# A fixed order for three engines in the interleaved part of the MLPs, and seven products instead of eight for 7 of 8 K-pairs

## The chip, the cores and the metric

The kernel runs on one core of a Trainium2 chip. The metric is the device time of one execution in microseconds (us); lower is better. The engines are TensorE (PE, with PEld for its weight loads), VectorE (DVE), ScalarE (ACT), GpSimd (POOL) and SyncE (SP, which here only issues DMAs).

## What is computed

A decoder trunk of two layers over 256 tokens with 2048 features, in float32. Each layer is a mixer (the first one latent attention beside an mLSTM, the second one dilated attention) followed by a squared-ReLU MLP; a final norm ends it. The change touches the MLPs only:

```python
D_MODEL, SEQ, D_FF = 2048, 256, 8192

def squared_relu_mlp(h, w1, w2):
    return jnp.square(jax.nn.relu(h @ w1)) @ w2

for layer in range(2):
    x = x + mix(rms_norm(x, norm_mix[layer]))
    x = x + squared_relu_mlp(rms_norm(x, norm_mlp[layer]), mlp_w1[layer], mlp_w2[layer])
```

## The kernel before

**Split numbers.** Every float32 operand is split into a high and a low half (`halves`): ScalarE copies it into the type that TensorE multiplies (`wh`, line 135), VectorE subtracts that copy from the original (`wl`, line 136). A product is then three matmuls (`mm_three`: high by high, high by low, low by high). Weights arrive as 512 KB pieces (`wr`, line 127) through a ring of four buffers; `wh` and `wl` have rings of four too.

**The MLP.** D_FF is cut into four quarters (q). A quarter's hidden features are made in 16 blocks of 128 (`h`). A block is two halves, each with one weight piece, eight matmuls of 512 columns (line 164) and eight of 256 (line 168), all into PSUM bank 3. A block's result is copied out by ScalarE (`bt_h`), added up by VectorE (`hu`), put through ReLU and square by ScalarE, and stored for the second product: two blocks make a K-pair.

**The second product.** It runs over the 8 K-pairs of a quarter for one half of the 2048 output columns at a time; I call the work of one quarter and one column half a stretch. A K-pair can be multiplied with eight products (24 matmuls of 512 columns; `eight`, called twice a pair with 12 each) or, by Strassen's scheme in Winograd's form, with seven (21 matmuls; `seven`). For seven, VectorE first makes sums of weight pieces (`ta`, `tb`) and of activations (`hp`, then split into `pt`). A seven is two steps: the first (nine matmuls) goes into the PSUM tiles m1, m5, m7 (`ym`), the second (twelve) into m6 and three accumulators (`yc`, the output blocks 10, 01 and 00). The fourth accumulator, block 11, is only used by `eight`, and shares bank 3 with the `h` blocks. The four `ym` tiles come from a pool of four buffers. `SEVEN = 6` pairs go by seven, two by eight.

**The order before.** `woven` writes out one and a half seven-steps, then an `h` block, and so on: the twelve seven-steps of a stretch among eight `h` blocks that belong to the next stretch or to the next half of the quarter. Behind the last block come the four `eight` steps. Behind the last seven-step, `early_y` reads the four `ym` tiles (`yp`, `yq` are scratch) and adds to the residual `x`; behind the last eight, `late_y` adds the four accumulators to `x`. That is the order of writing; the framework's scheduler then orders each engine's queue by itself.

There are seven stretches in each layer (the eighth, at the end of each MLP, is written in another way). Layer 0's begin near 402 us, layer 1's near 1469 us.

Of the kernel before, what the change touches and what calls it, by code (L numbers as in the profile page):

```python
# [21 lines left out]
SEVEN = 6  # L22
# [47 lines left out]
def trunk(ctx: ExitStack, tc: tile.TileContext, plan, a, c_first, c_even, c_odd, out):  # L70
# [122 lines left out]
    def steps_seven(pool, H, pairs, w, c, early, late, name="y", hold=()):  # L193
# [12 lines left out]
        def seven(k):  # L206
# [8 lines left out]
            def go_a():  # L215
# [6 lines left out]
                ta = pool.tile([P, 2, 512], F32, name=f"ta{n_w[0]}", tag="ta", bufs=2)  # L222
# [40 lines left out]
        return [seven(k) for k in pairs], [[eight(k, j) for j in range(2)] for k in rest]  # L263

# [759 lines left out]
    def mlp(layer, norm, nxt):  # L1024
# [6 lines left out]
        def evac_h(H):  # L1031
            def make(c):
                box = {}

                def go(f, ac):
                    t = sm.tile([P, 512], F32, name="bt_h", tag="bt", bufs=2)
                    nc.scalar.activation(t, ac, AF.Copy)
                    u = sm.tile([P, S], F32, name="hu", tag="hu", bufs=2)
                    nc.vector.tensor_add(u, t[:, :S], t[:, S:])  # L1039
                    nc.scalar.activation(u, u, AF.Relu)  # L1040
                    if c >= SEVEN:
                        nc.scalar.activation(u, u, AF.Square)
                        H[2 * c + f] = sm.tile([P, 2, S], FR, name="ht", tag="ht", bufs=2 * (NF // 2 - SEVEN))
                        split_to(H[2 * c + f], u)
# [5 lines left out]
                    v = u.rearrange("p (b t) -> p b t", b=NB)  # L1050
                    nc.scalar.activation(dst, v, AF.Square)
                    if f == 1:
                        nc.vector.tensor_tensor(r[:, 4:6, :], r[:, 1:3, :], r[:, 2:4, :], OP.subtract)
                        nc.vector.tensor_tensor(r[:, 6, :], r[:, 5, :], r[:, 1, :], OP.subtract)
                        nc.vector.tensor_tensor(r[:, 7, :], r[:, 0, :], r[:, 6, :], OP.add)
                        pt = sm.tile([P, 2, 8, P], FR, name="pt", tag="pt", bufs=SEVEN)
                        nc.scalar.activation(pt[:, 0], r, AF.Copy)
                        nc.vector.tensor_tensor(pt[:, 1], r, pt[:, 0].bitcast(F32), OP.subtract)
                        H[2 * c], H[2 * c + 1] = (pt, 0), (pt, 1)
                return go  # L1060
            return make

        def early_y(c):
            def go(m1, m5, m6, m7):
                def add(b, j, src):
                    v = x[b][c + j]
                    nc.vector.scalar_tensor_tensor(v, src, scale["s"][:, b:b + 1], v, OP.mult, OP.add)

                p = sm.tile([P, 512], F32, name="yp", tag="yp", bufs=1)
                q = sm.tile([P, 512], F32, name="yq", tag="yq", bufs=1)  # L1070
                nc.scalar.activation(p, m1, AF.Copy)
                add(0, 0, m1)
                nc.vector.tensor_add(p, m6, p)
                nc.vector.tensor_add(q, m7, p)
                nc.vector.tensor_sub(p, m5, p)
                add(1, 0, q)
                nc.vector.tensor_sub(q, m5, q)
                add(0, 1, p)
                add(1, 1, q)
            return go  # L1080

        def late_y(c):
            def go(cc):
                for b, j in ((1, 1), (1, 0), (0, 1), (0, 0)):
                    v = x[b][c + j]
                    nc.vector.scalar_tensor_tensor(v, cc[b, j], scale["s"][:, b:b + 1], v, OP.mult, OP.add)
            return go

        def blocks(q, H):
# [3 lines left out]
            def block(i):  # L1093
                def go():
                    run(steps_feats(X, ("mlp_w1", layer, 0), q * (FF // NQ) + i * P,
                                    lambda f, ac: ev[i // 2](i % 2, ac), n=P, name="h", kt=8, bank=3))
                return go

            ev = [ev(c) for c in range(NF // 2)]
            return [block(i) for i in range(NF)], ev  # L1100

        H = [None] * NF
        hs, ev = blocks(0, H)
        steps = steps_feats(X, ("mlp_w1", layer, 0), 0, ev[0], name="h")
# [5 lines left out]
        for c in range(1, NF // 4):  # L1110
            run(steps_feats(X, ("mlp_w1", layer, 0), c * 256, ev[c], name="h"))
        for q in range(NQ):
            last = q == NQ - 1
            wq = ("mlp_w2", layer, q * (FF // NQ))
            seven, eight = steps_seven(sm, H, list(range(SEVEN)), wq, 0, early_y(0), late_y(0))
            woven(hs[NF // 2:], sum(seven, []))
            run(*eight)
            if last and nxt is None:
                finish(H, wq, early_y(2), scale, sm)
                break  # L1120
            pairs = list(range(3 if last else SEVEN))
            seven, eight = steps_seven(sm, H, pairs, wq, 1024, early_y(2), late_y(2))
            if last:
                nxt.stats(0)
                nxt.stats(1)
                steps = sum([a + b for a, b in zip(seven, eight)] + eight[len(seven):], [])
# [74 lines left out]
```

## Time and profile before

| | |
|---|---|
| time, three runs | 2115.13, 2117.52, 2119.45 us (median 2117.52) |
| profiled execution | 2115.02 us, span of the trace 2113.2 us |
| TensorE busy | 2093.8 us, 99% of the span |
| VectorE busy | 1742.3 us, 82% (90% or more in most slices of the MLPs) |
| ScalarE busy | 1303.7 us, 62% |
| granted TensorE clock | 0.999 of full |
| DMA | 404.5 MB, mean 191 GB/s |

A matmul's bar in the trace holds its way through the array, so the bars of matmuls that follow each other overlap. How long a run of matmuls takes is read from the starts, not from the bars; the same holds, with less overlap, for VectorE.

### The profile page before, as it was taken

The page shows a single profiled execution, that of the slowest core. Times are in us where ns is not written, and L with a number is a line of the kernel's source. Part 1 is how long each engine was busy: PE and PEld are TensorE (multiplying, and loading weights), DVE is VectorE, ACT ScalarE, POOL GpSimd, SP SyncE. Part 2 cuts the span into 40 slices and gives each one's busy share as a digit, 9 for nine tenths or more (in the row PEclk, how much of TensorE's full clock was granted, in tenths as well). Part 3 has the DMA queues.
Part 4 walks back from the last instruction along what each step waited for, and adds up shares of the span by engine and source line. Part 5 has one row for each costly group of instructions (what it writes and reads, how often), then busy time and mean ns, then how long its engine had stood idle before and what let it go on. Part 6 is the DMA issues. An engine that isn't in the chain of part 4 may idle for free.

```text
span 2113.2 us, 29343 instructions
## 1 busy us (share of the span) xinstructions
PE 2093.8 (99%) x10860; PEld 1797.8 (85%) x10860; DVE 1742.3 (82%) x2455; ACT 1303.7 (62%) x1876; POOL 6.1 (0%) x13
## 2 busy tenths in 40 slices
PE   9999999999999999999999999999999999999998
PEld 8998888888888888888888888888888888888886
DVE  5678555889999999999877667568899998999998
ACT  6575445766676666667544444457666666667665
POOL 0000000000000000000000000000000000000000
PEclk9999999999999999999999999999999999999999
DMA  8554455556565566566665555455565665656664
GB/s 295 165 174 158 160 176 187 178 191 216 183 211 197 190 202 204 192 205 195 197 194 174 170 179 170 163 186 178 193 205 194 206 201 188 204 194 200 203 213 162
DMA packets 115296, 404.51 MB, mean 191 GB/s; under 512 B 12944, under 2 KB 13584, under 8 KB 115152
## 3 DMA queue, kind: packets, MB, share of 16 engines
q1 hardware_dynamic: 114048, 400.02, 57.9%
q8 instruction: 85, 1.39, 0.3%
q0 software_dynamic: 384, 1.51, 0.2%
q10 hardware_dynamic: 720, 1.11, 0.1%
q14 instruction: 59, 0.48, 0.1%
HBM read 400.49 MB, written 2.10 MB: 191 GB/s over the span
## 4 chain that ended last, share of the span: by engine, by line
PE 88%; DVE 7%; DMA 2%; issue 1%; ACT 1%; SPq 0%; POOLq 0%; POOL 0%; DVEq 0%; ACTq 0%
PE h L164 21%; PE h L168 11%; PE yc L155 4%; PE yc L156 4%; PE yc L154 4%; PE ym L155 4%; PE ym L156 3%; PE ym L154 3%; DVE wl L136 3%; PE k L164 3%; PE o L154 3%; PE o L156 3%; PE o L155 3%; PE q L164 3%; PE v L154 2%; PE v L156 2%
## 5 line engine op out<-in xcount | busy, mean ns | idle before, releaser
L136 DVE TENSOR_TENSOR wl<-wr,wh 128x1024 fp32r<-128x1024 f32 (+4 forms) x769 | 865.6, 1134 | 259.8 <-ACT wh L135 254.5
L135 ACT ACTIVATE wh<-wr 128x1024 fp32r<-128x1024 f32 (+4 forms) x769 | 753.8, 986 | 515.6 <-PE h L164 136.6
L164 PE MATMUL h<-T,wh 128*128 128x512 f32 x2048 | 511.4, 392 | 1.1 <-ACT wh L135 0.9
L164 PEld LDWEIGHTS h<-T,wh 128*128 128x128 f32 x2048 | 374.5, 188 | 76.0 <-ACT wh L135 2.6
L168 PEld LDWEIGHTS h<-T,wl 128*128 128x128 f32 x2048 | 279.3, 190 | 20.1
L168 PE MATMUL h<-T,wl 128*128 128x256 f32 x2048 | 285.5, 282 | 0.0
L155 PE MATMUL ym<-wl,pt 128*128 128x512 f32 x360 | 142.2, 395 | 1.8 <-DVE wl L136 1.8
L154 PE MATMUL ym<-wh,pt 128*128 128x512 f32 x360 | 140.1, 394 | 0.2 <-ACT wh L135 0.2
L156 PE MATMUL ym<-wh,pt 128*128 128x512 f32 x360 | 140.2, 389 | 0.0
L224 DVE TENSOR_TENSOR ta<-wr,wr 128x1024 f32<-128x1024 f32 x90 | 110.1, 1223 | 33.1 <-DMA wr<-in_mlp_w 32.4
L135 ACT ACTIVATE wh<-ta 128x1024 fp32r<-128x1024 f32 x90 | 95.2, 1058 | 61.0 <-DVE ta L224 60.9
L155 PE MATMUL yc<-wl,pt 128*128 128x512 f32 x318 | 124.0, 390 | 0.0
L154 PE MATMUL yc<-wh,pt 128*128 128x512 f32 x318 | 123.2, 390 | 0.0
L156 PE MATMUL yc<-wh,pt 128*128 128x512 f32 x318 | 122.8, 389 | 0.0
L1040 ACT ACTIVATE hu<-hu 128x256 f32<-128x256 f32 x128 | 52.6, 415 | 99.5 <-DVE hu L1039 99.3
L135 ACT ACTIVATE wh<-tb 128x1024 fp32r<-128x1024 f32 x90 | 94.7, 1052 | 28.5 <-DVE tb L226 28.3
L136 DVE TENSOR_TENSOR wl<-tb,wh 128x1024 fp32r<-128x1024 f32 x90 | 109.7, 1219 | 1.9 <-ACT wh L135 1.7
L136 DVE TENSOR_TENSOR wl<-ta,wh 128x1024 fp32r<-128x1024 f32 x90 | 109.7, 1219 | 0.0
L154 PE MATMUL o<-wh,M 128*128 128x512 f32 x256 | 102.3, 399 | 0.0
L156 PE MATMUL o<-wh,M 128*128 128x512 f32 x256 | 99.8, 390 | 0.0
L155 PE MATMUL o<-wl,M 128*128 128x512 f32 x256 | 99.7, 389 | 0.0
L154 PE MATMUL yc<-wh,ht 128*128 128x512 f32 (+1 forms) x256 | 99.4, 388 | 0.0
(297 smaller groups left out, 3320.9 us busy)
## 6 DMA issues: line engine op xcount, KB each, us to landing
wr<-in_mlp_w SPq DMA_DIRECT2D x512, 512.0 KB, 4.1
wr<-in_od_w_qkv SPq DMA_DIRECT2D x96, 512.0 KB, 4.1
wr<-in_ev_w_in SPq DMA_DIRECT2D x32, 512.0 KB, 3.5
wr<-in_ev_w_out SPq DMA_DIRECT2D x32, 512.0 KB, 3.4
wr<-in_od_w_out SPq DMA_DIRECT2D x32, 512.0 KB, 3.5
wr<-in_ev_w_in SPq DMA_DIRECT2D x24, 344.0 KB, 3.1
wr<-in_ev_w_in SPq DMA_DIRECT2D x15, 364.0 KB, 5.8
wr<-in_mla_w_ukv SPq DMA_DIRECT2D x8, 512.0 KB, 3.7
```

The costliest lines, as they stand in the source:

```text
L135: nc.scalar.activation(hi, raw, AF.Copy)
L136: nc.vector.tensor_tensor(lo, raw, hi.bitcast(F32), OP.subtract)
L154: nc.tensor.matmul(ac, xh, hi, start=first, stop=False)
L155: nc.tensor.matmul(ac, xh, lo, start=False, stop=False)
L156: nc.tensor.matmul(ac, xl, hi, start=False, stop=last)
L164: nc.tensor.matmul(acs[f], hi[:, j, f * P:(f + 1) * P], Ts[j].rearrange("p a t -> p (a t)"), start=first and j == 0, stop=False)
L168: nc.tensor.matmul(acs[f][:, :S], lo[:, j, f * P:(f + 1) * P], Ts[j][:, 0, :], start=False, stop=last and j == n - 1)
L224: nc.vector.tensor_tensor(ta, r0, r1[:, 0:1, :].to_broadcast([P, 2, 512]), OP.add)
L1040: nc.scalar.activation(u, u, AF.Relu)
```

## The change

`SEVEN` is 7, `ta` has one buffer instead of two (in the old form of the second product as well), and the seven stretches of a layer are written as a list of units whose order is fixed for ScalarE, VectorE and TensorE: the scheduler no longer moves their instructions. The lines that carry it:

```diff
-SEVEN = 6
+SEVEN = 7
...
+    def drive(units, left):
+        ahead = [(n, kind, f) for n, u in enumerate(units) for kind, f in u.prep]
+        due = {}
+        for n, u in enumerate(units):
+            first, rest = due.pop(n, ([], []))
+            splits = []
+            while ahead and left.get(ahead[0][1], 1) > 0:
+                _, kind, f = ahead.pop(0)
+                if kind:
+                    left[kind] -= 1
+                splits.append(f)
+            run(first, [f for pair in zip(splits, rest) for f in pair], splits[len(rest):], rest[len(splits):])
+            for d, now, f in u.go() or ():
+                due.setdefault(n + d, ([], []))[not now].append(f)
+            for kind in u.free:
+                left[kind] += 1
...
+            return [Unit([(None, sums), ("w", split(0, lambda: t["r0"])), ("t", split(1, lambda: t["ta"], pool, "t", 3))],
+                         go_a, ["t"]),
+                    Unit([("w", split(3, lambda: t["r1"][:, 1:2, :])),
+                          ("t", split(2, lambda: t["tb"], pool, "t", 3))], go_b, ["w", "w", "t"])]
...
+                due = [(1, True, copy), (1, False, add), (2, False, square)]
+                if c >= SEVEN:
+                    return due + [(3, False, plain)]
+                return due + ([(3, False, sums), (4, False, pair)] if f == 1 else [])
...
+                return [(1, True, both(nc.scalar.activation, p, m1, AF.Copy)),
+                        (1, True, add(0, 0, m1)),
+                        (1, False, both(nc.vector.tensor_add, p, m6, p)),
+                        (1, False, both(nc.vector.tensor_add, q, m7, p)),
+                        (2, False, both(nc.vector.tensor_sub, p, m5, p)),
+                        (2, False, add(1, 0, q)),
+                        (3, False, both(nc.vector.tensor_sub, q, m5, q)),
+                        (3, False, add(0, 1, p)),
+                        (4, False, add(1, 1, q))]
...
-                for b, j in ((1, 1), (1, 0), (0, 1), (0, 0)):
+                return [(1, True, add(b, j)) for b, j in ((1, 0), (0, 1), (0, 0), (1, 1))]
...
-            woven(hs[NF // 2:], sum(seven, []))
-            run(*eight)
+        pattern = "shshshhshshhshs"
+                for what in pattern:
+                    units += (seven if what == "s" else hs).pop(0)
+                units += eight
+        with tc.manual_schedule(engines={mybir.EngineType.PE, mybir.EngineType.Activation, mybir.EngineType.DVE}):
+            drive(units, {"w": 4, "t": 3})
```

`drive` goes through the units. Ahead of each it writes out what came due (`first`, then the others in turn with the splits for coming units), as many splits as there are free buffers of either kind, then the unit's matmuls. A unit returns what follows from it, with the number of units after which it is due. A stretch is now: seven, block, seven, block, seven, two blocks, seven, block, seven, two blocks, seven, block, seven, two eights. I name its units s0a, s0b (the two steps of the first seven), h0a, h0b (the halves of the block behind it), and so on to s6a, s6b, e0, e1, and then s0a of the next stretch.

**VectorE between two stretches, before.** This is the end of layer 0's fourth stretch (a second column half), from the first early addition on: the splits for the two halves of the `h` block that stands behind the last seven (`wl_7104`, `wl_7126`), the other early additions (lines 1067 to 1077; `ym_6428` is m5), and the first of the splits for the four `eight` steps (`wl_7160`).

```order
L1067 SCALAR_TENSOR_TENSOR x_75<-ym_6427,iv_mlp_3681,x_75 128x512
L136 TENSOR_TENSOR wl_7104<-wr_7101,wh_7103 128x1024
L136 TENSOR_TENSOR wl_7126<-wr_7123,wh_7125 128x1024
L1039 TENSOR_TENSOR hu<-bt_h 128x256
L1073 TENSOR_TENSOR yp<-ym_6430,yp 128x512
L1074 TENSOR_TENSOR yq<-ym_6429,yp 128x512
L1075 TENSOR_TENSOR yp<-ym_6428,yp 128x512
L1067 SCALAR_TENSOR_TENSOR x_79<-yq,iv_mlp_3681,x_79 128x512
L1067 SCALAR_TENSOR_TENSOR x_76<-yp,iv_mlp_3681,x_76 128x512
L1077 TENSOR_TENSOR yq<-ym_6428,yq 128x512
L136 TENSOR_TENSOR wl_7160<-wr_7157,wh_7159 128x1024
L1067 SCALAR_TENSOR_TENSOR x_80<-yq,iv_mlp_3681,x_80 128x512
```

The early additions stand close together, with m5's last reading (the second `yq`) among them. Three more eights' splits and the next stretch's first sums and split follow, and only then the late additions.

**VectorE between two stretches, now.** This is the same place, from the first early addition (due after `s6b`) on; the splits of e0 and e1, one `hu` and s0's sums (`ta`, twice `tb`) stand ahead of it. `wl_7246`, `wl_7253`, `wl_7258` and `wl_7263` are the splits of s0's four pieces (`wr_7209`, `ta`, `wr_7211`, `tb`) in the next stretch, `wl_7281` is that of h0a. The bracket names the engines whose semaphores a row waits for.

```order
L1195 SCALAR_TENSOR_TENSOR x_75<-ym_6506,iv_mlp_3681,x_75 128x512 [waits Activation_49]
L136 TENSOR_TENSOR wl_7246<-wr_7209,wh_7245 128x1024 [waits Activation_49]
L1171 TENSOR_TENSOR hp<-hp 128x256
L1172 TENSOR_TENSOR hp<-hp 128x128 [waits DVE_49]
L1173 TENSOR_TENSOR hp<-hp 128x128 [waits DVE_49]
L136 TENSOR_TENSOR wl_7253<-ta_7213,wh_7252 128x1024 [waits Activation_49]
L1198 TENSOR_TENSOR yp<-ym_6509,yp 128x512
L136 TENSOR_TENSOR wl_7258<-wr_7211,wh_7257 128x512 [waits Activation_49]
L1198 TENSOR_TENSOR yq<-ym_6508,yp 128x512 [waits DVE_49]
L136 TENSOR_TENSOR wl_7263<-tb_7214,wh_7262 128x1024 [waits Activation_49]
L136 TENSOR_TENSOR wl_7281<-wr_7278,wh_7280 128x1024 [waits DMAHW7_49,Activation_49]
L1179 TENSOR_TENSOR pt<-hp,pt 128x1024 [waits Activation_49]
```

The early additions that stood together are now spread among splits, and the `hp` sums and the `pt` split of the last pair stand among them too. The rows that follow without a gap are these: the rest of m5's first reading (`ym_6507` is m5), the four late additions (line 1215), the split of h0b (`wl_7309`), and m5's second reading.

```order
L1198 TENSOR_TENSOR yp<-ym_6507,yp 128x512 [waits DVE_49]
L1195 SCALAR_TENSOR_TENSOR x_79<-yq,iv_mlp_3681,x_79 128x512
L1215 SCALAR_TENSOR_TENSOR x_79<-yc_6520,iv_mlp_3681,x_79 128x512 [waits DVE_49,PE_49]
L1215 SCALAR_TENSOR_TENSOR x_76<-yc_6521,iv_mlp_3681,x_76 128x512 [waits PE_49]
L1215 SCALAR_TENSOR_TENSOR x_75<-yc_6522,iv_mlp_3681,x_75 128x512
L1215 SCALAR_TENSOR_TENSOR x_80<-yc_7289,iv_mlp_3681,x_80 128x512 [waits PE_49]
L136 TENSOR_TENSOR wl_7309<-wr_7306,wh_7308 128x1024 [waits DMAHW0_49,Activation_49]
L1198 TENSOR_TENSOR yq<-ym_6507,yq 128x512
```

The four late additions now stand ahead of m5's second reading. At the end of a first column half the rows are the same, but for one `ht` row where `hp` (three rows) and `pt` (one) stand here.

**TensorE there, now.** These are the last matmuls of s0a in the next stretch (m5 as `ym_7324`, m7 as `ym_7325`), and the first of s0b (m6 as `ym_7326`, then the accumulator of block 10).

```order
L154 MATMUL ym_7324<-wh_7252,pt 128x512 [waits DVE_49,Activation_49]
L155 MATMUL ym_7324<-wl_7253,pt 128x512
L156 MATMUL ym_7324<-wh_7252,pt 128x512
L154 MATMUL ym_7325<-wh_7252,pt 128x512 [waits DVE_49]
L155 MATMUL ym_7325<-wl_7253,pt 128x512
L156 MATMUL ym_7325<-wh_7252,pt 128x512
L154 MATMUL ym_7326<-wh_7262,pt 128x512 [waits DVE_49,Activation_49]
L155 MATMUL ym_7326<-wl_7263,pt 128x512
L156 MATMUL ym_7326<-wh_7262,pt 128x512
L154 MATMUL yc_7337<-wh_7262,pt 128x512
```

The first matmul into m6 waits for VectorE, and no later one in s0b, h0a or h0b waits for VectorE again, though h0b's low half (`wl_7309`) and the freeing of bank 3 (the last late addition) are needed there.

## Rows read from the trace of the kernel before

**Rows 1.** The page, part 1: engine, busy us, share, instructions.
```profile
PE 2093.8 (99%) x10860; PEld 1797.8 (85%) x10860; DVE 1742.3 (82%) x2455; ACT 1303.7 (62%) x1876; POOL 6.1 (0%) x13
```

**Rows 2.** Windows: one stretch of layer 0's MLP, then the end; PEclk is the granted clock.
```profile
core 0: us, PE busy (x) PEld busy (x) DVE busy (x) ACT busy (x) POOL busy (x), PEclk, DMA share, GB/s
649.00:734.00 85.00, 84.55 (x431) 71.81 (x431) 79.18 (x97) 55.11 (x73) 0.00 (x0) 1.00 0.60 200
...
2106.00:2107.00 1.00, 0.00 (x0) 0.00 (x0) 0.16 (x2) 0.51 (x2) 0.12 (x1) 0.97 0.05 18
2107.00:2108.00 1.00, 0.00 (x0) 0.00 (x0) 0.53 (x2) 0.53 (x1) 0.43 (x1) 0.50 0.00 0
```

**Rows 3.** Groups by line and shape, 402 to 990 us.
```profile
L156 PE MATMUL ym<-wh,pt 128*128 128x512 f32 x168 | 65.4, 389 | 0.0
```

**Rows 4.** Timeline of TensorE in layer 0's MLP: start, duration, instruction.
```profile
729.98 0.40 PE L155 MATMUL yc<-wl,ht 128*128 128x512 f32 x1
...
735.44 0.39 PE L155 MATMUL yc<-wl,ht 128*128 128x512 f32 x1
...
746.56 2.00 PE L164 MATMUL h<-T,wh 128*128 128x512 f32 x8
...
749.35 2.00 PE L164 MATMUL h<-T,wh 128*128 128x512 f32 x8
```

**Rows 5.** The chain that ended last, in order of time: start, duration, work.
```profile
1627.62 4.32 DMA wr<-in_mlp_w
...
1967.34 4.30 DMA wr<-in_mlp_w
```

**Rows 6.** Timeline of VectorE at the end of a column half.
```profile
707.96 1.23 DVE L224 TENSOR_TENSOR ta<-wr,wr 128x1024 f32<-128x1024 f32 x1 [0.64 <-DMA wr<-in_mlp_w]
...
710.55 1.22 DVE L136 TENSOR_TENSOR wl<-wr,wh 128x1024 fp32r<-128x1024 f32 x1
...
712.82 0.69 DVE L136 TENSOR_TENSOR wl<-wr,wh 128x512 fp32r<-128x512 f32 x1
713.42 0.42 DVE L1039 TENSOR_TENSOR hu<-bt_h 128x256 f32<-128x256 f32 x1
713.76 1.22 DVE L136 TENSOR_TENSOR wl<-tb,wh 128x1024 fp32r<-128x1024 f32 x1
714.90 0.42 DVE L1053 TENSOR_TENSOR hp<-hp 128x256 f32<-128x256 f32 x1
...
715.88 2.35 DVE L136 TENSOR_TENSOR wl<-wr,wh 128x1024 fp32r<-128x1024 f32 x2
718.15 1.22 DVE L1058 TENSOR_TENSOR pt<-hp,pt 128x1024 fp32r<-128x1024 f32 x1
719.29 0.75 DVE L1067 SCALAR_TENSOR_TENSOR x<-ym,iv_mlp,x 128x512 f32<-128x512 f32 x1
719.95 1.22 DVE L136 TENSOR_TENSOR wl<-wr,wh 128x1024 fp32r<-128x1024 f32 x1
```

**Rows 7.** Timeline of ScalarE there.
```profile
720.68 1.06 ACT L135 ACTIVATE wh<-wr 128x1024 fp32r<-128x1024 f32 x1 [1.67 <-PE h L164]
721.65 0.58 ACT L1037 ACTIVATE bt_h<-h 128x512 f32<-128x512 f32 x1
```

**Rows 8.** Timeline of TensorE at the start of the program.
```profile
4.44 0.98 PE L154 MATMUL c<-wh,T 128*128 128x364 f32 x2 [4.44 <-ACT wh L135]
...
8.15 0.51 PE L155 MATMUL c<-wl,T 128*128 128x364 f32 x1
8.45 0.51 PE L156 MATMUL c<-wh,T 128*128 128x364 f32 x1
...
11.22 0.33 PE L155 MATMUL c<-wl,T 128*128 128x364 f32 x1
11.39 0.33 PE L156 MATMUL c<-wh,T 128*128 128x364 f32 x1
```

**Rows 9.** Timeline of TensorE at its end.
```profile
2104.68 0.28 PE L156 MATMUL z<-wh,ht 128*128 128x256 f32 x1
```

More of the change, by code (lines that the diff above doesn't have):

```diff
@@ L1031, in evac_h, with make, copy, add @@
         def evac_h(H):
[L1032 to L1039, printed above, removed]
+            boxes = [{} for _ in range(NF // 2)]
+            def make(i, ac):
+                c, f = divmod(i, 2)
+                box = boxes[c]
+                def copy():
+                    box["t"] = sm.tile([P, 512], F32, name="bt_h", tag="bt", bufs=2)
+                    nc.scalar.activation(box["t"], ac, AF.Copy)
+                def add():
+                    t = box["t"]
+                    box["u"] = sm.tile([P, S], F32, name="hu", tag="hu", bufs=2)
+                    nc.vector.tensor_add(box["u"], t[:, :S], t[:, S:])
+                def square():
+                    u = box["u"]
                     nc.scalar.activation(u, u, AF.Relu)
@@ L1091, in blocks, with at_once, units_h, unit @@
+            return due
+        def at_once(f):
+            return lambda *arg: run([go for _, _, go in f(*arg)])
+        w1 = ("mlp_w1", layer, 0)
+        def units_h(q, H, blocks):
             ev = evac_h(H)
-            def block(i):
+            def unit(i, g, box):
+                t = {}
+                def split():
+                    t["w"] = weights(w1, 8 * g, 8, q * (FF // NQ) + i * P, P)
                 def go():
-                    run(steps_feats(X, ("mlp_w1", layer, 0), q * (FF // NQ) + i * P,
-                                    lambda f, ac: ev[i // 2](i % 2, ac), n=P, name="h", kt=8, bank=3))
-                return go
@@ L1099, in blocks @@
-            ev = [ev(c) for c in range(NF // 2)]
-            return [block(i) for i in range(NF)], ev
+                    if g == 0:
+                        box["a"] = acc("h", 3)
+                    mm_feats([box["a"]], [X[k] for k in range(8 * g, 8 * g + 8)], *t["w"], g == 0, g == 1)
+                    if g == 1:
+                        return ev(i, box["a"])
+                return Unit([("w", split)], go, ["w"])
+            out = []
+            for i in blocks:
+                box = {}
+                out.append([unit(i, g, box) for g in range(2)])
@@ L1102, in mlp, with evac @@
+            return out
         H = [None] * NF
-        hs, ev = blocks(0, H)
-        steps = steps_feats(X, ("mlp_w1", layer, 0), 0, ev[0], name="h")
+        ev = evac_h(H)
+        def evac(c):
+            return lambda f, ac: run([go for _, _, go in ev(2 * c + f, ac)])
+        steps = steps_feats(X, w1, 0, evac(0), name="h")
         run(steps[:3])
```

159 lines of the change are left out of this document (108 added, 51 removed).

## The prediction

> **What bounds the kernel now.** I read the engines' shares first. TensorE is busy 99% of the span, VectorE 82%, ScalarE 62% [rows 1]. In a stretch of the MLP (a quarter's work for one column half) VectorE is busy 79.18 of 85.00 us, at a granted clock of 1.00 [rows 2]. So TensorE sets the pace there and VectorE has about 6 us in hand. Next comes the price of TensorE's work, and the bars mislead: a 512-column matmul's bar is 389 ns [rows 3], but from 729.98 to 735.44 there are 24 starts, 0.2275 us each, and half an `h` block takes 749.35 − 746.56 = 2.79 us [rows 4]. Then the length of a stretch: the chain shows a load at the same place of the loop every second stretch, and from 1627.62 to 1967.34 lie four of them, 84.93 us each [rows 5]. Full speed would be 16 × 2.79 + (6 × 21 + 2 × 24) × 0.2275 = 84.23 us. TensorE loses 0.7 us a stretch, no more.
>
> **What the change takes away.** Three matmuls for each of 14 stretches, 42 in all: 42 × 0.2275 = 9.6 us. A stretch at full speed is now 16 × 2.79 + (7 × 21 + 24) × 0.2275 = 83.54 us. By the bars it would have been 42 × 0.389 = 16.3 us. [...]
>
> **What it adds on VectorE.** From start to start, a piece of 1024 columns costs 1.14 us (718.15 to 719.29), 512 columns 0.60 (712.82), 256 columns 0.34 (713.42), a seven's three sums 2.59 in a row (707.96 to 710.55), the `hp` sums 0.98 (714.90 to 715.88), an addition to `x` 0.66 (719.29) [rows 6]. The seventh pair costs 2.59 + 3 × 1.14 + 0.60 = 6.61 where the eight cost 2 × 1.14, so +4.3 us a stretch. Its activations, once in two stretches, cost 0.98 + 1.14 instead of 2 × 0.34, so +0.7 a stretch. VectorE's work in a stretch becomes 79.2 + 5.0 = 84.2 us, against 83.5 on TensorE. ScalarE, at 55 of 85 us [rows 2], has room for its one and a half more splits. The DMA pieces are as many as before, in the same order. The reserve of 6 us is gone, so the order has to hide everything.
>
> **What it moves.** Before, a block and four eights stood between the last seven of a stretch and the next stretch's first: 2 × 2.79 + 48 × 0.2275 = 16.5 us, in which VectorE did the early additions. Now it is e0 and e1: 24 × 0.2275 = 5.46 us. I walk through this place, with time 0 at the end of s6b.
> - *TensorE* would do e0 and e1 until 5.46, s0a (9 matmuls) until 7.51, and then start s0b with m6.
> - *What s0b waits for.* The rows of TensorE's list say it: the first matmul into m6 waits for VectorE, and nothing behind it waits for h0b's `wl` or for bank 3 to be read. So that one wait covers VectorE's list down to the last `yq`, m5's second reading, which gives the buffer back. In between stand four late additions, which need e1's result.
> - *When VectorE gets there.* h7's last half ends 4.78 us (21 matmuls) before 0. Then ScalarE copies the block out, 0.58, and makes e1's high half, 1.06 [rows 7]; VectorE does e1's `wl`, a `hu` and s0's sums, 1.14 + 0.34 + 2.59. That is 5.71 us, and VectorE is at the first early addition at 0.9, if it never lagged before. From there to the last `yq` the list has six additions (4.0), five pieces of 1024 and `pt` (6.8), five of 512 (3.0) and `hp` (1.0): 14.8 us, so 15.7. VectorE's rows ran in list order in the old trace too (the addition and the `wl` at 719.29 and 719.95 stand so in its list).
> - *The stall.* 15.7 − 7.5 = 8.2 us of idle TensorE at the end of a second column half. At the end of a first one `hp` and `pt` (2.1) are replaced by an `ht` (0.34): 6.4 us, part of it already inside e0, which waits for that `ht`.
>
> Bounds: below, even a VectorE far ahead can do the late additions only after 5.46, and 4 × 0.66 + 1.14 + 0.60 = 4.4 us must follow while TensorE has 2.05 us of s0a, so 2.3 us at least. Nearer, s0's first `wl` can't end before about 1.5, since its buffer is read until 0.7 us before 0 and 1.06 and 1.14 follow; that would leave 7.0 and 5.2. Above there is no bound but a lag that VectorE brings along; the stall itself gives it time to get ahead again, so I add none. I take 8.2 and 6.4, six times each. Behind each layer's last stretch the scheduler orders again; the early and late additions stand together with s0's splits there, and between 2.3 and 8 I take 5.5, twice. Sum: 49.2 + 38.4 + 11.0 = 98.6 us.
>
> **The rest of the stretch.** From the end of a block's half, 0.58 + 1.06 + 1.14 + 0.98 + 2.59 + 0.34 + 1.14 us of copy, splits and sums fit before the next seven needs them 10.4 us later, almost without spare. So I leave the old 0.7 us a stretch, but take off 0.5 for each of the 12 crossings, as the old loss that sat there is replaced: −6. The single `ta` buffer costs nothing in the fixed part, where the next sums stand behind the last split of the old `ta` in VectorE's list anyway; without that cover it would be some tenths.
>
> **The clock.** In the old trace TensorE never stops for long inside the span. At the end, the last matmul starts at 2104.68 [rows 9] and the granted clock falls from 1.00 to 0.50 (1.2 GHz) near 2106.9 [rows 2]. At the start, matmuls of 364 columns follow each other at 0.30 us (8.15, 8.45) and later at 0.17 (11.22, 11.39), with the first at 4.44 [rows 8]: some 6.5 us at half speed. A stall of 6 to 8 us may do the same here. Bounds: nothing, or half of 6.5, 3.3 us, a crossing. No trace has a stop of middle length, so I take 1.7 for 12 crossings, 20 us. The Trainium skill ("TensorE: Matmul & The Clock Gate", HAM oscillation — how this bites in real kernels) tells of a kernel whose every wait for data put the clock back to half. By that rule every crossing would pay (a rival, below). No stop inside this trace shows it; its end agrees.
>
> **Sum.** 2115.0 (the profiled execution: span 2113.2 and 1.8 around it) − 9.6 + 98.6 − 6 + 20 = 2218 us. The median of the runs lies 2.5 above the profiled one, so 2221.
>
> **The rivals.**
> - *The clock stays up.* As above without the 20 us: 2200. For it: no stop of this kind is in the trace. Against it: the end of the span.
> - *VectorE as plain bound, with small stalls.* If the scheduler's list is misread and the crossings cost only the 2.3 us that are certain, 14 × 2.3 − 9.6 − 6 gives 2134. If VectorE's 84.2 us also keep half of the old 5.8 us of waits, a stretch is 87.1, and 2115 + 14 × (87.1 − 84.9) + 2.5 gives 2148. For it: 84.2 exceeds 83.5. Against it: the late additions stand ahead of what s0b needs.
> - *Faster.* The place is m6's buffer. If s0b's first matmul were released by an earlier reading than m5's last one, and late additions were done by 7.5, each stretch would run at 83.5 and a little more: 2117.5 − 9.6, and −6 at best, so 2102 to 2108. It decides as soon as VectorE reaches the last `yq` at 7.5, eight us earlier than I have it. Against it: e1 ends at 5.46.
> - *The order changes nothing* and only the matmuls go: the lists differ at every crossing, so this falls together with the case above.
> - *The clock costs its whole 3.3 us at each of 14 crossings*, 46 us: 2247, and up to 2275 if VectorE also comes a little late each time. For it: the fall came only 2 us after the last matmul. Against it: at the end of a first half the stop is in two parts. The Trainium skill's rule on the clock gate, named above, stands for this case.
>
> **How the numbers follow.** Long stalls with a lowered clock, 2205 to 2245: 0.46. Long stalls with the clock up, 2180 to 2205: 0.22. Small stalls, 2130 to 2180: 0.16. The clock in full, over 2245: 0.11. Faster or equal: 0.05. The predicted time is 2221 us. For the range I leave out the upper part of that last case and most of the small stalls: 2165 to 2255. Within 0.2% (about what a measurement of this kernel can tell from no change) would need an accident between the cases: 0.01. Faster by more than that: 0.04. Slower: 0.95.
>
> **What will show it.** Right: 12 idle gaps of TensorE of 5 to 8 us, each ended by VectorE at a `ym` matmul (line 154) a little behind the eights, some 92 us apart and alternately longer and shorter; VectorE without a pause before each; 42 matmuls fewer; the mean granted clock under 0.99. Wrong: gaps spread among the sevens inside a stretch (then VectorE's sum is the bound), or stretches near 83.5 us (then VectorE had the lead that I deny it).

## The result and the profile after

| | before | after |
|---|---|---|
| time, median (lowest to highest) | 2117.99 us (2115.13 to 2119.45, 4 runs) | 2300.1 us (2299.05 to 2303.04, 4 runs) |
| ratio | | 1.0864 [1.0845, 1.0883], slower |
| span of the profiled execution | 2113.2 us | 2297.2 us |
| granted TensorE clock, mean | 0.999 | 0.975 |
| matmuls | 10860 | 10818 |

The change costs 182 us. The direction was forecast; 2300 lies above the range of 2165 to 2255. The whole difference is in the two MLPs: from the start of the first `h` matmul to the end of the last `yc` one, layer 0's lasts 681.1 us before and 772.9 after, layer 1's 680.1 and 771.2. Everything else is as it was within about 1 us.

The page, part 1, and the engines' line of its part 4 (the chain that ended last), of after:

```profile
PE 2146.3 (93%) x10818; PEld 1812.5 (79%) x10818; DVE 1824.5 (79%) x2541; ACT 1317.7 (57%) x1896; POOL 6.1 (0%) x13
...
PE 62%; DVE 22%; ACT 6%; issue 5%; DMA 4%; DVEq 0%; SPq 0%; ACTq 0%; POOLq 0%; POOL 0%
```

Beside [rows 1], TensorE has gone from 99% to 93% of its span, and VectorE, with 82 us more to do, from 82% to 79%. No engine is full any more: they wait for each other in turn. The chain says so too, with 22% of the span on VectorE.

Next the waits of the whole execution of after (engine, line it waits at, releaser: us in all, times, longest). The `PE` rows are those that matter:

```profile
ACT hu L1155 <- DVE hu L1151: 172.9, 104, 2.6
...
PE ym L154 <- DVE yq L1198: 69.6, 17, 8.4
...
PE h L164 <- ACT bt_h L1146: 25.7, 28, 1.0
...
PE yc L156 <- DVE ht L407: 11.7, 6, 2.3
...
PE ym L154 <- DVE yp L1198: 9.8, 6, 1.9
...
PE yc L154 <- ACT ht L406: 8.6, 8, 1.1
```

I call the place between one stretch's last seven and the next one's first a crossing; the fixed order has 12. Four of the five `PE` rows are theirs, but for two of the eight `ht` waits of line 406 (1.03 and 1.02 us), which stand behind the two layers' last stretches: 69.6 + 9.8 + 11.7 + 8.6 − 2.1 = 97.6 us. The fifth, 28 times about 0.9 us, is something else: two `h` blocks next to each other (below). In the kernel before, TensorE waited once for a block's copy:

```profile
PE h L164 <- ACT bt_h L1037: 0.2, 1, 0.2
```

Two stretches in windows (the answer to [rows 2]). Their borders are the starts of a load at the same place of the loop in the chain, as in [rows 5]:

```profile
575.94:676.50 100.56, 88.22 (x428) 73.27 (x427) 85.92 (x105) 57.63 (x77) 0.00 (x0) 0.95 0.53 169
676.50:774.16 97.66, 88.72 (x429) 73.34 (x428) 83.87 (x101) 56.62 (x76) 0.00 (x0) 0.97 0.54 171
```

A stretch lasts 99.1 us on average instead of 84.93. VectorE is busy for 84.9 of them, close to the 84.2 that were added up; so it has 14 us to spare, and its sum is not the bound. The granted clock is 0.95 and 0.97.

TensorE at the end of a second column half (timeline: start, duration, instruction, in brackets the idle time before and its releaser). The first row is the first matmul of e0, so s6b ends at 579.71, the zero of the prediction's walk:

```profile
579.71 0.39 PE L154 MATMUL yc<-wh,ht 128*128 128x512 f32 x1
...
585.15 0.39 PE L154 MATMUL ym<-wh,pt 128*128 128x512 f32 x1
...
587.79 0.47 PE L154 MATMUL ym<-wh,pt 128*128 128x512 f32 x1 [1.80 <-DVE yp L1198]
...
588.90 0.50 PE L154 MATMUL ym<-wh,pt 128*128 128x512 f32 x1 [0.18 <-DVE yq L1198]
...
598.22 0.77 PE L154 MATMUL ym<-wh,pt 128*128 128x512 f32 x1 [8.35 <-DVE yq L1198]
598.78 0.63 PE L155 MATMUL ym<-wl,pt 128*128 128x512 f32 x1
599.21 0.63 PE L156 MATMUL ym<-wh,pt 128*128 128x512 f32 x1
```

e0 and e1 take 5.44 us (forecast 5.46). Then s0a's second and third product wait 1.80 and 0.18, and s0b's first matmul, the one into m6, waits 8.35. Behind it the starts lie 0.43 us apart where [rows 4] have 0.2275: half clock.

VectorE in the same place:

```profile
579.23 0.42 DVE L1151 TENSOR_TENSOR hu<-bt_h 128x256 f32<-128x256 f32 x1
580.45 1.23 DVE L314 TENSOR_TENSOR ta<-wr,wr 128x1024 f32<-128x1024 f32 x1 [0.80 <-DMA wr<-in_mlp_w]
...
583.04 0.75 DVE L1195 SCALAR_TENSOR_TENSOR x<-ym,iv_mlp,x 128x512 f32<-128x512 f32 x1
...
593.61 2.73 DVE L1215 SCALAR_TENSOR_TENSOR x<-yc,iv_mlp,x 128x512 f32<-128x512 f32 x4
...
597.39 0.68 DVE L1198 TENSOR_TENSOR yq<-ym,yq 128x512 f32<-128x512 f32 x1
597.99 1.21 DVE L314 TENSOR_TENSOR ta<-wr,wr 128x1024 f32<-128x1024 f32 x1
```

From the first early addition (583.04) to the end of the last `yq` (597.99) are 14.95 us, without a pause, as listed (14.8). But VectorE is at that addition 3.3 us after s6b's end, not 0.9.

At the end of a first column half (same view; s6b ends at 680.29) the stop is in three parts, 6.78 us together:

```profile
680.29 0.39 PE L154 MATMUL yc<-wh,ht 128*128 128x512 f32 x1
...
682.91 0.50 PE L154 MATMUL yc<-wh,ht 128*128 128x512 f32 x1 [1.09 <-ACT ht L406]
685.77 0.50 PE L156 MATMUL yc<-wh,ht 128*128 128x512 f32 x1 [2.13 <-DVE ht L407]
...
696.89 0.77 PE L154 MATMUL ym<-wh,pt 128*128 128x512 f32 x1 [3.56 <-DVE yq L1198]
```

VectorE comes to its first early addition 3.2 us after s6b's end there too:

```profile
683.51 0.74 DVE L1195 SCALAR_TENSOR_TENSOR x<-ym,iv_mlp,x 128x512 f32<-128x512 f32 x1
```

The six stops of the second column halves are 10.0 us on average, those of the first ones 6.2.

And two neighbouring blocks in the middle of a stretch (same view):

```profile
631.31 2.11 PE L164 MATMUL h<-T,wh 128*128 128x512 f32 x8 [1.00 <-ACT bt_h L1146]
```

That is the second block's first row; it goes into bank 3 too, so it waits until ScalarE has copied the first one out.

### The profile page after: what moved, and what is told of

Read it like the earlier page. It is cut to its first block, busy times and chain, and to the rows that moved or that the text cites. A ratio compares the mean times of both kernels' runs of the same rounds, so it can differ in the third digit from the quotient of the medians.

```text
span 2297.2 us, 29345 instructions
## 1 busy us (share of the span) xinstructions
PE 2146.3 (93%) x10818; PEld 1812.5 (79%) x10818; DVE 1824.5 (79%) x2541; ACT 1317.7 (57%) x1896; POOL 6.1 (0%) x13
## 4 chain that ended last, share of the span: by engine, by line
PE 62%; DVE 22%; ACT 6%; issue 5%; DMA 4%; DVEq 0%; SPq 0%; ACTq 0%; POOLq 0%; POOL 0%
PE h L164 13%; DVE wl L136 10%; PE h L168 6%; ACT wh L135 4%; DMA wr<-in_mlp_w 4%; DVE ta L314 3%; PE k L164 3%; PE o L156 3%; PE o L154 3%; PE o L155 3%; PE q L164 3%; PE yc L156 2%; PE yc L155 2%; PE yc L154 2%; PE v L154 2%
## 5 line engine op out<-in xcount | busy, mean ns | idle before, releaser
L164 PE MATMUL h<-T,wh 128*128 128x512 f32 x2048 | 516.2, 394 | 25.7 <-ACT bt_h L1146 25.7
L154 PE MATMUL ym<-wh,pt 128*128 128x512 f32 x416 | 167.8, 406 | 80.1 <-DVE yq L1198 69.6
L155 PE MATMUL ym<-wl,pt 128*128 128x512 f32 x416 | 170.0, 409 | 6.5 <-DVE wl L136 4.0
L156 PE MATMUL ym<-wh,pt 128*128 128x512 f32 x416 | 165.1, 397 | 0.0
L154 PEld LDWEIGHTS ym<-wh,pt 128*128 128x128 f32 x416 | 79.4, 191 | 105.6 <-issue 73.8
L155 PE MATMUL yc<-wl,pt 128*128 128x512 f32 x376 | 152.1, 405 | 0.4 <-DVE wl L136 0.4
L1155 ACT ACTIVATE hu<-hu 128x256 f32<-128x256 f32 x128 | 52.8, 415 | 172.9 <-DVE hu L1151 172.9
L154 PE MATMUL yc<-wh,pt 128*128 128x512 f32 x376 | 151.1, 406 | 0.7 <-DVE x L1215 0.5
L156 PE MATMUL yc<-wh,pt 128*128 128x512 f32 x376 | 151.7, 404 | 0.0
L1146 ACT ACTIVATE bt_h<-h 128x512 f32<-128x512 f32 x128 | 74.7, 590 | 102.6 <-PE h L168 102.6
L136 DVE TENSOR_TENSOR wl<-ta,wh 128x1024 fp32r<-128x1024 f32 x104 | 126.7, 1218 | 0.4 <-ACT wh L135 0.4
L136 DVE TENSOR_TENSOR wl<-tb,wh 128x1024 fp32r<-128x1024 f32 x104 | 126.5, 1217 | 0.4 <-ACT wh L135 0.3
L155 PEld LDWEIGHTS ym<-wl,pt 128*128 128x128 f32 x416 | 79.8, 192 | 33.2 <-DVE wl L136 22.2
L154 PE MATMUL o<-wh,M 128*128 128x512 f32 x256 | 102.3, 399 | 0.0
```

Source lines behind the costliest of these rows:

```text
L136: nc.vector.tensor_tensor(lo, raw, hi.bitcast(F32), OP.subtract)
L154: nc.tensor.matmul(ac, xh, hi, start=first, stop=False)
L155: nc.tensor.matmul(ac, xh, lo, start=False, stop=False)
L156: nc.tensor.matmul(ac, xl, hi, start=False, stop=last)
L164: nc.tensor.matmul(acs[f], hi[:, j, f * P:(f + 1) * P], Ts[j].rearrange("p a t -> p (a t)"), start=first and j == 0, stop=False)
L1146: nc.scalar.activation(box["t"], ac, AF.Copy)
```

## The experiments

Unless a ratio stands there, a time is one profiled execution; the kernel before took 2117 to 2118 us beside each. e1 and e2 take the change apart, the others move rows or units.

**e1: the seventh pair (with the single `ta` buffer) alone, order left to the scheduler.**

```diff
(kernel before)
-SEVEN = 6
+SEVEN = 7
-... name=f"ta{n_w[0]}", tag="ta", bufs=2)
+... name=f"ta{n_w[0]}", tag="ta", bufs=1)
```

> The kernel before with the seventh pair and the single ta buffer, but without the fixed order: the scheduler orders all queues as before. Theory (the fixed order at the crossings is what costs): no long stops of TensorE at the crossings, a stretch of 84 to 87 us, 2105 to 2150 us in all. Rival (VectorE's 5 us more a stretch are what costs, in whatever order): 2240 us or more, with VectorE's share near 100% of a stretch.

Measured: 2153.25 us (2148.77 to 2157.81, 4 runs), ratio 1.0169 [1.0148, 1.0189]; clock 0.998. Its waits of TensorE:

```profile
PE h L164 <- ACT wh L135: 14.8, 10, 2.5
```

The seventh pair and the single `ta` buffer cost 35 us and not 182. The scheduler keeps the crossing free of long stops (no `yq` row at all). What is left is splits that come a little late; the rows name ScalarE's high halves, and whether VectorE's missing reserve stands behind that they do not show. The time is slightly above the expected range's upper end.

**e2: the fixed order alone, with six sevens.**

```diff
(kernel after)
-SEVEN = 7
+SEVEN = 6
-        pattern = "shshshhshshhshs"
+        pattern = "shshshhshhshhs"
```

> The changed kernel with 6 of 8 pairs by seven and the pattern shshshhshhshhs, so four eights (10.92 us) stand between the last seven and the next stretch, in the fixed order. Theory (the 5.46 us between s6 and the next s0 were too short for what stands in VectorE's list): m5's last reading now comes ahead of the late additions, the stops of 4 to 8.4 us are gone and the clock stays up; left are about 0.9 us at each of three double blocks a stretch. A stretch of 87 to 89 us, 2145 to 2175 us in all. Rival (the fixed order is slow by itself, since ScalarE and VectorE wait for each other in it): 2220 us or more.

Measured: 2236.08 us, clock 0.986. The theory misses, and the rival has it: the fixed order with six sevens (and the single `ta` buffer) costs 118 us. Its waits of TensorE:

```profile
PE h L164 <- ACT bt_h L1146: 40.6, 42, 1.8
PE yc L154 <- DVE x L1215: 28.9, 14, 2.4
...
PE ym L154 <- DVE yq L1198: 5.9, 6, 1.0
```

Here `yq` is nearly gone, since four eights stand in the crossing. But this order of units has three pairs of neighbouring blocks a stretch, 42 in all, each about a microsecond; and s0b's second product waits for the late additions. So the six-pair case has other stops of the same sort. The four corners: scheduler and six 2118, scheduler and seven 2153, fixed and six 2236, fixed and seven 2300; 35 and 118 make 153 of the 182, and 29 arise only with both.

**e3: m5's last reading one unit earlier.** If the stop is where the last `yq` stands in VectorE's list, moving that row ahead of the late additions must shorten it.

```diff
(kernel after)
-                        (3, False, both(nc.vector.tensor_sub, q, m5, q)),
+                        (2, False, both(nc.vector.tensor_sub, q, m5, q)),
```

> The changed kernel with m5's second reading due one unit earlier, ahead of the four late additions and of h0b's split. Theory (m6's first matmul waits for just that row): the long stop shrinks by 4 x 0.66 + 1.14 = 3.8 us less a little, from 8.4 to about 4.6 at one kind of crossing and from 3.6 to near 0 at the other, and the clock falls for less time; 2235 to 2260 us. Rival (the late additions bind the accumulators of s0b anyway, or the wait is for another row): the stop only moves to the next matmuls, 2290 to 2305 us.

Measured: 2265.14 us, clock 0.981: 35 us less, a little short of the expected range. Its `yq` row of the waits, then the stop at the same crossing as above (TensorE) and the row that ends it (VectorE):

```profile
PE ym L154 <- DVE yq L1198: 28.4, 14, 4.5
```

```profile
592.95 0.77 PE L154 MATMUL ym<-wh,pt 128*128 128x512 f32 x1 [4.02 <-DVE yq L1198]
...
592.11 0.69 DVE L1198 TENSOR_TENSOR yq<-ym,yq 128x512 f32<-128x512 f32 x1
592.72 2.72 DVE L1215 SCALAR_TENSOR_TENSOR x<-yc,iv_mlp,x 128x512 f32<-128x512 f32 x4
```

The late additions now stand behind the `yq`, and the stop is 4.02 instead of 8.35. All `yq` waits fall from 69.6 to 28.4, the block pairs rise from 25.7 to 32.3.

**e4: the square one unit later**, and with it the `hp` sums and `pt`; it takes two rows out of the way of ScalarE's splits for s6.

```diff
(kernel after)
-                due = [(1, True, copy), (1, False, add), (2, False, square)]
+                due = [(1, True, copy), (1, False, add), (2 if c >= SEVEN else 3, False, square)]
...
-                return due + ([(3, False, sums), (4, False, pair)] if f == 1 else [])
+                return due + ([(4, False, sums), (5, False, pair)] if f == 1 else [])
```

> The changed kernel with ReLU and square of a block that goes into a seven due one unit later (and so its hp sums and its pt split). In ScalarE's list the high half of a seven's first piece then stands ahead of a ReLU that waits for VectorE, and at the crossing pt's split stands behind m5's last reading. Theory (VectorE reaches the crossing 3 us late because ScalarE stood behind rows that wait for VectorE): the first early addition comes 2 to 3 us sooner after s6b, and the stop of 8.4 us falls to 4 to 6; 2255 to 2280 us. Rival (VectorE is late because its sum of work is too long): the first early addition comes as late as before, only pt's 1.1 us are won at six or seven crossings, 2288 to 2300 us.

Measured: 2300.89 us, clock 0.970: no gain, and just outside both expected ranges. VectorE came only 0.8 us sooner, to the first early addition 2.5 us after s6b's end (581.46 − 578.94) instead of 3.3. But s1's sums and `pt` now stand ahead of the last `yq`, and the list from there on takes 17.5 us instead of 14.95. The stop follows the row's place in the list, now to the other side:

```profile
PE ym L154 <- DVE yq L1198: 98.8, 18, 11.9
```

**e5: in the second column half, blocks behind the last seven.** With two blocks there, 16.6 us of TensorE's work lie in the crossing instead of 5.5. For the first half this can't be written: e0 needs the last two blocks themselves.

```diff
(kernel after)
-        pattern = "shshshhshshhshs"
...
-                for what in pattern:
+                for what in "shshshhshshhshs" if c == 0 else "shshshshshshshh":
```

> The changed kernel, but in the stretches of the second column half the order is seven and block in turn, and two blocks stand behind the last seven (one pair of neighbouring blocks there instead of two), so that 16.6 us instead of 5.5 us of TensorE's work lie between a stretch's last seven and the next first one. Theory (the stop is VectorE's list between the last seven and the last yq, done in too little time): at the six such crossings the stop of about 8.4 us and its half clock (about 2 us) go, a block pair's wait (0.9 us) goes with them, the first-half crossings stay: 2225 to 2250. Rival (VectorE's sum of work per stretch is the bound, and the waits only move into the sevens): 2280 to 2305.

Measured: 2236.12 us, clock 0.986: 64 us less, as the theory has it. Waits of TensorE:

```profile
PE h L164 <- ACT bt_h L1146: 25.2, 22, 2.2
PE ym L154 <- DVE yq L1198: 23.5, 6, 5.2
...
PE ym L155 <- DVE wl L136: 8.4, 14, 1.5
```

Only six `yq` waits are left, one for each first-half crossing. The `bt_h` waits follow the number of neighbouring blocks: 22 pairs and 22 waits here, 28 in after, 42 in e2. VectorE does the same work per stretch (1822.3 us busy over the span), so its sum is not the bound. The waits moved into the sevens are 8.4 us.

**e6: the same, and m5's last reading earlier.**

```diff
(e5)
-                        (3, False, both(nc.vector.tensor_sub, q, m5, q)),
+                        (2, False, both(nc.vector.tensor_sub, q, m5, q)),
```

> The same order, and besides m5's last reading (yq) one unit earlier in the lists, which shortens the stop at the first-half crossings too. Theory: another 25 to 40 us less, 2190 to 2220, with the rest of the loss at the neighbouring blocks and the plain ht behind the last block. Rival (VectorE's sum is the bound): no change against the order alone, within 10 us of it.

Measured: 2222.58 us, clock 0.992. The `yq` wait is gone (2.9 us), but only 13.5 us are won, half of what the theory wanted, since another product now waits for a block's copy, which it did for 3.3 us in e5:

```profile
PE yc L154 <- ACT bt_h L1146: 9.8, 6, 1.7
```

What remains beyond the kernel before, 105 us, is without long stops at all: block pairs 24.7 and 9.8, the plain `ht` behind the last block 20.5, late splits 9.1, half clock 13.6 (matmuls that start late at a granted clock near 0.50), and smaller delays.

**e7: a light crossing.** The order of units is that of after; the rows that no buffer waits for are moved behind the last `yq`.

```diff
(kernel after)
-                return due + ([(3, False, sums), (4, False, pair)] if f == 1 else [])
+                late = 3 if i == 7 else 0
+                return due + ([(3 + late, False, sums), (4 + late, False, pair)] if f == 1 else [])
...
-                        (1, True, add(0, 0, m1)),
+                        (2, False, add(0, 0, m1)),
...
-                        (3, False, both(nc.vector.tensor_sub, q, m5, q)),
-                        (3, False, add(0, 1, p)),
-                        (4, False, add(1, 1, q))]
+                        (2, False, both(nc.vector.tensor_sub, q, m5, q)),
+                        (5, False, add(0, 1, p)),
+                        (6, False, add(1, 1, q))]
```

> The changed kernel's order of blocks and sevens, but the lists of the crossing are made light: m5's last reading one unit earlier, the early additions to x that no buffer waits for and the last block's sums and splits moved behind it, so that VectorE's list from s0's first split to the last yq takes about 9.9 us instead of 14.8. Theory: the yq stop goes to about a third of its 72 us, the clock falls less often, 2215 to 2245. Rival (what is moved back only makes a later wait, in s0b or at the first block): 2260 to 2300.

Measured: 2249.26 us, clock 0.984, 4 us above the expected range. The rows of the same crossing:

```profile
585.53 0.47 PE L154 MATMUL ym<-wh,pt 128*128 128x512 f32 x1 [0.80 <-DVE yq L1199]
...
588.97 0.51 PE L154 MATMUL ym<-wh,pt 128*128 128x512 f32 x1 [2.50 <-DVE x L1196]
...
591.04 0.77 PE L154 MATMUL ym<-wh,pt 128*128 128x512 f32 x1 [1.01 <-DVE yq L1199]
```

10.3 us of stops have become 4.3. What is new is 2.50 at s0a's third product: the addition from m1, which was moved back, holds a buffer as well. The theory holds for the place, the rival for a part of the gain.

**e8: `hu` ahead of the next sums.** I took ScalarE's wait for `hu` (its ReLU row waits 172.9 us in all) to be the reason why VectorE reaches the crossing late.

```diff
(kernel after)
-                due = [(1, True, copy), (1, False, add), (2, False, square)]
+                due = [(1, True, copy), (1, True, add), (2, False, square)]
```

> The changed kernel with one flag changed: VectorE makes hu ahead of the next seven's sums instead of behind them, so ScalarE's ReLU waits less and comes to the split behind it sooner. Theory (VectorE starts its crossing list some 3 us later than I had it, because ScalarE's list is held up by that hu): VectorE is at the first early addition 1 to 2 us sooner, the stops shorten by that much: 2270 to 2290. Rival (the lateness comes from the pieces and DMAs, or the sums pushed back make the splits late): 2295 to 2320.

Measured: 2290.39 us. That is at the edge of the theory's range, but the step behind the theory fails: the first early addition still comes 3.1 us after s6b's end (583.73 − 580.67), and the `yq` waits are 72.5 us instead of 69.6. That row is not what makes VectorE late. ScalarE's wait has moved to the next row of its list, the square ahead of s6's splits (after, then e8):

```profile
571.55 0.42 ACT L1163 ACTIVATE hp<-hu 128x256 f32<-128x256 f32 x1 [0.78 <-DVE pt L1179]
...
572.49 0.42 ACT L1163 ACTIVATE hp<-hu 128x256 f32<-128x256 f32 x1 [2.35 <-DVE pt L1179]
```

In after 1.80 us for `hu` stand ahead of that 0.78; in e8 they are gone, and the square waits 2.35. It writes `hp`, which has one buffer, and VectorE still reads the pair before from it for `pt`, behind s6's sums in its list. No run gives `hp` a second buffer, so what this wait costs in all is not shown.

**e10: the order of e6 with `hu` first** (e8's line in e6's kernel).

> The order with two blocks behind the second half's last seven, m5's last reading one unit earlier, and hu ahead of the next sums. Theory: the yq wait is gone already, so only the lateness of ScalarE's copies and splits can gain: 2205 to 2222, the block pairs (25 us) and the plain ht behind the last block (20 us) stay. Rival (ScalarE's and VectorE's lists wait for each other all along the stretch, and hu is the row that holds them): under 2195.

Measured: 2200.73 us, clock 0.993, between the two expected ranges. The blocks' waits went from 34.5 to 20.3 us (`PE h` alone now), and there is the most of the 22 us. It is the fastest kernel with seven sevens in the fixed order, and 83 us above the kernel before.

**e9: six sevens, seven and block in turn.** This asks whether the 118 us of e2 belong to a fixed order as such.

```diff
(kernel after)
-SEVEN = 7
+SEVEN = 6
-        pattern = "shshshhshshhshs"
+        pattern = "shshshshshshhh"
```

> Fixed order with six sevens, but another order of units: seven and block in turn, and three blocks behind the last seven (two pairs of neighbouring blocks a stretch instead of three, 27.7 us of TensorE's work between a stretch's last seven and the next first one instead of 11). Theory (the fixed order as such costs nothing; what costs is how little stands at the crossing, and two blocks next to each other): the wait of s0b for the late additions goes, the pairs keep 28 x 1.0 us, little half clock: 2150 to 2180. Rival (a list fixed by hand makes the engines wait for each other's rows whatever the order of the units): 2205 to 2240, as the first fixed order with six (2236).

Measured: 2216.92 us, clock 0.985: the rival's number. The waits, though, are new ones that this order of units makes itself: in the first column half only one seven and one block stand between block 11 and s5, which needs blocks 10 and 11 and waits for their `pt`:

```profile
PE ym L156 <- DVE pt L1179: 25.5, 8, 3.3
PE h L164 <- ACT bt_h L1146: 19.2, 28, 0.7
```

So it decides nothing by itself, except that the late additions' wait is gone (28.9 to 2.1), as expected.

**e11: the same with that pair moved ahead.**

```diff
(e9)
-        pattern = "shshshshshshhh"
...
-                for what in pattern:
+                for what in "shshshhshshshh" if c == 0 else "shshshshshshhh":
```

> Fixed order with six sevens as in the run before it, but in the first column half the neighbouring blocks are 10 and 11 in the middle and 14 and 15 behind the last seven, so that the pair's split (pt) for s5 stands four units further ahead. Theory (the new wait of that run, 30 us for pt, came only from where block 11 stood; the fixed order as such costs nothing beyond the block pairs, 28 x 0.7 to 1.0 us, some plain ht and the clock): 2155 to 2190. Rival (a list fixed by hand makes the engines wait for each other wherever the units stand): 2205 to 2230, with the waits at another tile.

Measured: 2171.99 us, clock 0.995, in the theory's range. Waits of TensorE:

```profile
PE h L164 <- ACT bt_h L1146: 25.5, 28, 1.8
PE yc L154 <- ACT ht L406: 12.0, 6, 2.0
```

The `pt` wait is gone and 45 us with it. 64 of e2's 118 us came from where the units stood. Of the 54 that stay, the rows name block pairs (25.5) and plain `ht` (12.0 here and 3.6 at its low half); half clock adds 7.5.

**e12: the same with m5's reading earlier and `hu` first** (the two lines of e10 in e11's kernel). In this kernel block 14's place in the second product is filled from block 15's `hu`: both keep it under one name, and with `hu` first the second of two neighbouring plain blocks replaces it before the first has used it.

> The same, with m5's last reading one unit earlier and hu ahead of the sums. Theory: with six sevens no yq wait is left, so within 15 us of the run beside it, 2145 to 2185; a fixed order does not get below the kernel before, whose TensorE loses 0.7 us a stretch and never has two blocks next to each other. Rival: under 2118.

Measured: 2150.16 us, clock 0.999. Because one operand hangs on another row than it should, I use this time only for what it says without that: still 33 us above the kernel before.

## Why the prediction was right in direction and short in size

A wait in the profile begins where a matmul's bar ends, about 0.16 us (0.39 − 0.2275) behind the place of the next start. So the measured column is counted from start to start: how much later each matmul of the two MLPs starts than the one before it and the full-speed price (0.2275 us for 512 columns, 0.121 for 256) allow.

| term of the sum | forecast, us | measured, us | from |
|---|---|---|---|
| 42 matmuls | −9.6 | −9.6 | 10860 and 10818 on the page |
| stops at the 12 crossings | 87.6 | 103.6 | 35 waits, 97.6 in the profile's rows |
| the two last stretches | 11.0 | 8.3 | waits for `ht`, `x` and `wl` there |
| half clock | 20 | 35.7 | late starts at a granted clock near 0.50 |
| neighbouring blocks | none | 30.1 | 28 waits of `PE h` for `bt_h`, 25.7 in the rows |
| rest of the stretches | −6 | 14.7 | all other late starts: 25.4 after, 10.7 before |
| together | 103 | 183 | |

*The stops* were the main term, and their mechanism held: the place (s0b's first matmul, m6's buffer, m5's last `yq`) and the list of 14.8 us. e3, e4 and e7 move that row in VectorE's list and the stop follows, down and up; e5 gives the crossing more TensorE work and it disappears there. In the profile's rows a second-half crossing stops 10.0 us where 8.2 were forecast, and a first-half one 6.2 where 6.4 were. The second agreement is partly luck: VectorE was 2.3 us later than in the walk there too, so s0b starts 9.1 us late (696.89 against 680.29 + 7.51), but TensorE lost 2.2 of these in e0 and e1 without a recorded wait, most of it at half clock.

*VectorE's arrival* was put 2.4 us too early (0.9 against 3.3). In the trace ScalarE makes five splits for s6 back to back and copies block 7 out only behind them. VectorE's `wl` for e1 therefore ends at −0.5 where the walk has −2.0, and 0.80 more go into a wait for a weight piece. That ScalarE's wait for `hu` is the deeper reason was my theory after the result, and e8 refuted it: with `hu` early, the wait for `pt` and the one `hp` buffer took its place. What else makes ScalarE that late stays open.

*The clock* was sized at little more than half of what it did. In after, 173 matmuls start late at a granted clock near 0.50 without a recorded wait, 18.0 and 17.7 us in the two MLPs, and none before: 35.7 us, 3.0 for each of 12 crossings, near the upper bound of 3.3 that I gave and did not take. The rival "the clock costs its whole 3.3 us at each of 14 crossings" was nearly right in the price. No run keeps the clock up with the same stops, so the price is read from the starts alone.

*The step that failed* is "The rest of the stretch". It left the old 0.7 us a stretch, took 6 us off, and asked only whether the copy, splits and sums behind a block fit before the next seven (its own sum, 7.8 us of 10.4, leaves 2.6, more than its "almost without spare" says). It did not ask what the order puts next to each other. The pattern has "hh" twice in a stretch, and the blocks share one bank: 28 waits of 0.92 us in the rows, 30.1 us from start to start, that [rows 4] could not show, since there a block's start follows half a block without a gap, and the old order has no two blocks in a row. e2 shows the same per pair (42 times, 40.6 us). No run puts two neighbouring blocks into different banks; that the bank is the reason rests on the rows, where ScalarE's copy ends each of these waits, and on their number, which follows the pairs in after, e2 and e5. Nor did the step allow for the small delays: instead of 6 us less, the rest costs 14.7 more than before. In after 145 starts at full clock come up to a few tenths of a microsecond late, 19.9 us in all; 30 of them are matmuls with a low half in a seven's first step (7.4), 66 stand right behind a wait (7.4).

Against the forecast the neighbouring blocks are 30.1 us more, the rest of the stretches 20.7, the crossings 16.0 and the clock 15.7; the two last stretches are 2.7 less. That is the whole difference of 80 us.

*The rivals.* VectorE as plain bound: refuted by e5, which takes away 64 us and leaves VectorE's work as it is. Faster, through an earlier release of m6's buffer: refuted by the 8.35 us behind the last `yq`. That a fixed order costs something whatever the number of sevens was no rival of mine, and e2 shows that it is the larger part of the loss (118 of 182 us); e11 shows that more than half of it is where this list puts its units.

## What to carry to other kernels

When an order is fixed by hand, read for each place not only how long the work between two uses of a buffer lasts but in whose queue the releasing row stands and what stands ahead of it: here one row behind four others lengthened twelve stops. Look at the order for neighbours that share a bank, too, even where the old trace shows no wait. And price a stop with what follows it: in the kernels here with seven pairs in the fixed order the loss was 1.3 to 1.6 times the recorded waits of TensorE in the MLPs (after: 182 us for 131).

## What the runs showed of the hardware

The granted clock did not fall for every wait. In after, around a crossing and at two neighbouring blocks (windows: us, busy and instructions of PE, PEld, DVE, ACT and POOL, granted clock, DMA share, GB/s):

```profile
592.00:594.00 2.00, 0.00 (x0) 0.00 (x0) 1.90 (x4) 0.00 (x0) 0.00 (x0) 1.00 0.81 260
594.00:596.00 2.00, 0.00 (x0) 0.00 (x0) 2.00 (x4) 0.00 (x0) 0.00 (x0) 0.52 0.01 2
...
602.00:604.00 2.00, 2.00 (x6) 1.54 (x6) 0.43 (x1) 1.52 (x2) 0.00 (x0) 0.50 0.00 0
604.00:606.00 2.00, 2.00 (x11) 1.66 (x10) 2.00 (x3) 2.00 (x4) 0.00 (x0) 0.92 0.16 23
630.00:632.00 2.00, 1.00 (x6) 0.70 (x5) 1.97 (x3) 2.00 (x4) 0.00 (x0) 1.00 0.72 240
```

TensorE's last matmul before the stop began at 589.47; the clock went to 0.50 (1.2 GHz) near 594 and was still there at 604, although TensorE had worked without a pause since 598.22. The wait of 1.00 us at 631 left it at 1.00 (2.4 GHz). In e6 a wait of 1.89 us for bank 3 was followed by half clock, though no wait in that run's MLPs is longer than 2.2 us (a timeline row, then a window):

```profile
617.96 2.73 PE L164 MATMUL h<-T,wh 128*128 128x512 f32 x8 [1.89 <-ACT bt_h L1146]
...
620.00:622.00 2.00, 2.00 (x10) 1.84 (x9) 2.00 (x4) 1.06 (x1) 0.00 (x0) 0.50 0.69 244
```

The Trainium skill ("TensorE: Matmul & The Clock Gate", HAM oscillation — how this bites in real kernels) tells of a kernel in which each wait for data puts the clock back to half. By that rule every crossing pays; the trace of after agrees for the crossings, each of which has matmuls at a granted clock of 0.50, and shows with the block pairs that a wait of a microsecond does not.
